# An encoder layer on one core: x also read transposed, the first four attention heads projected ahead of the norm

## The chip, the core and the metric

The kernel runs on one core of a Trainium2 chip. Its time is device time in microseconds (us) from launch to the last byte of the output. Engines are named as in the profile: PE is TensorE (matmuls; PEld is its weight load), ACT is ScalarE, DVE is VectorE, POOL is GpSimd, SP is the queue that issues the DMAs. The profile's clock starts with the span of one profiled execution; what lies between span and measured time is launch and end.

## What is computed

One layer over 256 tokens of 1024 numbers, all in float32. Cut to what matters here:

```python
xn = _rms_norm(x, norm1_g[i])                     # per token: x * rsqrt(mean(x^2)+eps) * gain
(a_x, a_g, b_q, b_k, b_v, c_q, c_kv, c_kpe,
 d_q, d_k, d_v, d_g, gate_logits) = jnp.split(xn @ w_in[i], IN_OFFSETS, axis=-1)
y_a = _rglru_mixer(a_x, a_g, ...)                 # conv, four gates, two linear scans
y_b = _diff_attention(b_q, b_k, b_v, ...)         # 8 heads; q and k are rms-normed per head
y_c = _mla(c_q, c_kv, c_kpe, ...)
y_d = _retention(d_q, d_k, d_v, d_g, ...)
merged = gates[0]*(y_a @ w_br_a) + gates[1]*(y_b @ w_br_b) + ...
x = x + merged @ w_out[i]
x = x + square(relu(_rms_norm(x, norm2_g) @ w_ff1)) @ w_ff2
x = x + sigmoid(_rms_norm(x, norm3_g) @ w_ple_gate) * (p @ w_ple_proj)
```

## The kernel before, in words

**Matmuls.** Every large product is done in three PE passes: both operands are split into a high part (rounded to PE's fp32r form) and a low part, and high*high, high*low and low*high are summed. x is split once into `xTh` and `xTl` (features on partitions). Weights stream from memory in tiles of 1 MB (`raw`, three buffers, `load`, issued on SP). `pieces` turns half a tile at a time into a high part `hi` (a copy on ACT; for some pieces a CAST on DVE) and a low part `lo` (a subtraction on DVE); there are NR = 5 buffers of each. `a_mode` makes 512 columns (or 384, 320) of tokens-by-features from two tiles, `b_mode` 256 features by tokens from one. Both end a tile with a call of `tick`.

**Stages, in program order.** First the norm: `rstd` of x on ACT, a scaling on DVE, 16 PE transposes (line 207 is `transpose`, line 194 is `mm`), the split into `xTh`/`xTl`. Then `a_in(0..3)` (the recurrence's input and its convolution `xc`), `b_in(0)` and `b_in(1)` (q, k, v of four heads each), `a_out(0..3)` (the recurrence's gelu branch; each needs its finished recurrence `ha[u]`), `c_in` (the latent projections: the first matmuls that are 384 columns wide), then gates, merges, the other branches, output, feed-forward and the last gate.

**Side work.** What is not a large product is written as generators: `a_mix(u)` (recurrence block u: gate matmuls `mm<-xc,bd` in plain float32, sigmoids, exp, tanh, square, square root, two scans), `b_rot` (head norm, rotation, transposes), `b_mix` (scores, softmax, weighted sum) and so on. `start` appends one to the list `side`; `tick` adds `pace` units of credit per tile (G0 = 3.0 in the first phase) and advances the first WIDTH = 4 generators whose `needs` are met until the credit is used up; each `yield` states its cost. Per generator these costs add up to 11.5 for an `a_mix`, 2.2 and 2.8 for a `b_rot` of q and of k, 9.8 for a `b_mix`. `finish(g)` runs g to its end at once. In the list the generators stand in the order in which they were started.

**Who orders the queues.** The tile framework places each instruction in its engine's queue by the order of the program, with priorities: loads and pieces are raised by AHEAD and AHEAD_S (60 instructions), the start by FIRST. After that each engine takes its own queue strictly as it stands, and waits on semaphores for what it needs. Accumulators `acc` are four PSUM banks, `mm` four more.

The main program of this phase is:

```python
for u in range(4):
    xc = a_in(u)
    if u == 0:
        derived_params()
    ...
    ga.append(start(a_mix(u, xc, ha[u])))
yb = yhl()
for c in range(2):
    for p, (...) in enumerate(b_in(c)):
        gb.append(start(b_mix(2 * c + p, ...), (r0, r1)))
pace[0] = G1
for u in range(4):
    finish(ga[u])
    a_out(u, ha[u], ya)
cs = c_in()
```

Of the kernel before, what the change touches and what calls it, by code (L numbers as in the profile page):

```python
# [14 lines left out]
P = 128  # L15
# [143 lines left out]
def _pack(w):  # L159
    import numpy as np  # L160

    return {'x': np.asarray(w['x']), 'weights': _pack_weights(w), 'params': _pack_params(w), 'lru': _pack_lru(w),
            'pT': np.ascontiguousarray(np.asarray(w['p'])[0, 0].T.reshape(2, P, S).transpose(1, 0, 2)),
            'gate_b': np.ascontiguousarray(np.asarray(w['gate_b'])[0]), 'decay': _decay()}

# [2 lines left out]
def encoder_kernel(ctx: ExitStack, tc: tile.TileContext, a, out):  # L168
# [50 lines left out]

    xs = const.tile([P, 2, D], F32, name="xs")  # L220
    par = const.tile([P, N_PAR], F32, name="par")
    with tc.high_priority(FIRST):
        for t in range(2):
            for c in range(2):
                w = slice(512 * c, 512 * c + 512)
                nc.sync.dma_start(xs[:, t, w], a['x'][0, t * P:(t + 1) * P, w])
        nc.sync.dma_start(par[:, :O_LATE], a['params'][:, :O_LATE])

    ident = const.tile([P, P], F32, name="ident")
    make_identity(nc, ident)  # L230
# [4 lines left out]
    act(eps[:, 2:3], eps[:, 0:1], AF.Sqrt)  # L235
    nhalf = const.tile([P, 16], F32, name="nhalf")
    nc.vector.memset(nhalf, -0.5)

# [9 lines left out]
    sp = const.tile([P, 2, 16], F32, name="sp")  # L248

    def derived_params():  # L250
        nc.sync.dma_start(par[:, O_LATE:], a['params'][:, O_LATE:])
# [45 lines left out]
    xTh = const.tile([P, 8, S], F32R, name="xTh")  # L297
    xTl = const.tile([P, 8, S], F32R, name="xTl")

    def rstd(src, scratch):  # L300

        st = small.tile([P, 2], F32, tag="nst", name="nst")
# [66 lines left out]
    def pieces(raw, o, n, alloc=None):  # L369
# [5 lines left out]
            hi, lo = alloc(), alloc()  # L375
        with tc.high_priority(AHEAD_S):
            count[0] += 1
            if count[0] % 2 == 0 and count[0] in V_HI:
                nc.vector.tensor_copy(out=hi[:, :n], in_=raw[:, o:o + n])
            else:  # L380
                act(hi[:, :n], raw[:, o:o + n], AF.Copy)
# [9 lines left out]
    def a_mode(xh, xl, name, KT, n0, nn, by_token=0):  # L391
# [4 lines left out]
        for k0 in range(0, KT, 4):  # L396
            kc = min(4, KT - k0)
            raw = load(name, k0 * P, n0)
            for p0 in range(0, kc, 2):
                kp = min(2, kc - p0)  # L400
                hi, lo = pieces(raw, p0 * nn, kp * nn)
                late = k0 >= KT - by_token
                for t in range(2):
# [37 lines left out]
    with tc.tile_pool(name="br", bufs=1) as br:  # L441
# [4 lines left out]
        def SH(name):  # L446
            return br.tile([P, 512], F32, tag="SH", name=name, bufs=NS)

        with tc.high_priority(FIRST):
            for t in range(2):  # L450
                r_ = rstd(xs[:, t, :], lambda: SH("xsq"))
                nc.vector.tensor_scalar(out=xs[:, t, :], in0=xs[:, t, :], scalar1=r_, scalar2=None, op0=MULT)
            for k2 in range(4):
                pt = mm_bank().rearrange("p (k s) -> p k s", s=S)
                for t in range(2):
# [3 lines left out]
                for k in range(2):  # L459
                    kk = 2 * k2 + k  # L460
                    split_scaled(xTh[:, kk, :], xTl[:, kk, :], pt[:, k, :], c1('norm1_g', kk))

        def y4():
            return br.tile([P, 4, S], F32R, tag="y4", name="y4", bufs=NY)
# [129 lines left out]
            split_scaled(*yw(yy, 2 * p), pair_T(lambda t, h: y[:, t, h, :]), gcol)  # L594


        def b_in(c):

            pairs = [[], []]
            for j, o0 in enumerate((O_BQ, O_BK, O_BV)):  # L600
                ps = a_full(xh, xl, W_in, 8, o0 + 512 * c, 512)
                for p in range(2):
                    x = (SH if j < 2 else L)("bx").rearrange("p (t c) -> p t c", t=2)
                    for t in range(2):
                        act(x[:, t, :], ps[t][:, 256 * p:256 * p + 256], AF.Copy)
# [486 lines left out]
```

## Time and profile before

| what | value |
|---|---|
| median of 3 runs | 736.91 us (736.8 to 738.08) |
| the profiled execution's own time | 736.86 us |
| its span | 735.1 us |
| granted TensorE clock, mean | 1.000 |
| PE busy | 718.0 us, 98% |
| DVE busy | 526.6 us, 72% |
| ACT busy | 428.2 us, 58% |
| first `a_out` matmul | 116.73 us |
| first 384-column matmul (`c_in`) | 140.62 us |

The table by engine says how much each engine worked in all; the windows say in which stretch; a timeline row gives start, length, engine, source line, operation, and in brackets how long the engine stood idle before it and what released it. PE lengths are pipelined and overlap, so rates are read from the starts of rows that follow each other.

### The profile page before, as it was taken

The numbers are of one execution on the slowest core, as the hardware profiler recorded it, in microseconds if no ns is written. First come the engines' busy times: TensorE is split into PE (matmuls) and PEld (weight loads), VectorE is DVE, ScalarE is ACT, GpSimd is POOL, SyncE is SP. The second block draws the span as 40 slices with busy tenths as digits, with TensorE's granted clock in tenths as the row PEclk, the third lists the DMA queues.
The fourth block names the chain that finished last, engine by engine and source line by source line (L and its number), as shares of the span: only waits on it lengthen the run. The fifth ranks groups of instructions, "written<-read, shape, count | busy, mean of one in ns | idle before, by whom it ended". The sixth has DMA issues, their size and how long they took to land.

```text
span 735.1 us, 10616 instructions
## 1 busy us (share of the span) xinstructions
PE 718.0 (98%) x4066; PEld 622.7 (85%) x4066; DVE 526.6 (72%) x893; ACT 428.2 (58%) x744; POOL 49.4 (7%) x58
## 2 busy tenths in 40 slices
PE   5999999999999999999999999999999999999997
PEld 4988889997888898888888888877899999888886
DVE  5988978998777879976775778576666666445652
ACT  7589867483745996556544444445755555445551
POOL 0000012222011033110000101000000000000000
PEclk9999999999999999999999999999999999999999
DMA  8754444365344254443555475543564455536611
GB/s 299 263 218 172 171 172 144 119 247 188 122 161 136 91 180 167 170 170 132 186 173 198 163 244 185 199 171 144 179 222 172 173 179 193 202 118 227 233 52 58
DMA packets 22802, 128.47 MB, mean 175 GB/s; under 512 B 2656, under 2 KB 2912, under 8 KB 9440
## 3 DMA queue, kind: packets, MB, share of 16 engines
q1 hardware_dynamic: 22752, 127.80, 48.8%
q8 instruction: 32, 0.52, 0.3%
q14 instruction: 18, 0.15, 0.1%
HBM read 126.74 MB, written 1.05 MB: 174 GB/s over the span
## 4 chain that ended last, share of the span: by engine, by line
PE 64%; DVE 1%; ACT 0%; issue 0%
PE acc L194 57%; PE mm L194 3%; PE mm L207 2%; PE mm L198 1%; ACT hi L191 0%; DVE lo L185 0%; DVE gate L188 0%; DVE pg L185 0%; DVE y L188 0%; DVE xs L185 0%; ACT pg L191 0%
## 5 line engine op out<-in xcount | busy, mean ns | idle before, releaser
L185 DVE TENSOR_TENSOR lo<-raw,hi 128x1024 fp32r<-128x1024 f32 (+3 forms) x226 | 268.3, 1192 | 119.3 <-ACT hi L191 118.8
L191 ACT ACTIVATE hi<-raw 128x1024 fp32r<-128x1024 f32 (+2 forms) x200 | 207.6, 1043 | 194.8 <-PE acc L194 166.0
L194 PE MATMUL acc<-hi,xTh 128*128 128x512 f32 (+3 forms) x376 | 146.3, 389 | 0.0
L194 PE MATMUL acc<-hi,y 128*128 128x512 f32 x448 | 144.5, 398 | 0.0
L194 PE MATMUL acc<-hi,xTl 128*128 128x512 f32 (+3 forms) x376 | 142.8, 380 | 0.0
L194 PE MATMUL acc<-lo,xTh 128*128 128x512 f32 (+3 forms) x376 | 142.6, 379 | 0.0
L194 PE MATMUL acc<-xTl,hi 128*128 128x256 f32 x384 | 109.1, 284 | 0.2 <-DVE xTl L188 0.2
L194 PE MATMUL acc<-xTh,hi 128*128 128x256 f32 x384 | 109.2, 286 | 0.0
L194 PE MATMUL acc<-xTh,lo 128*128 128x256 f32 x384 | 108.7, 284 | 0.0
L194 PEld LDWEIGHTS acc<-hi,y 128*128 128x128 f32 x448 | 84.2, 188 | 19.8
L194 PE MATMUL acc<-lo,y 128*128 128x512 f32 x224 | 89.0, 397 | 0.0
L194 PEld LDWEIGHTS acc<-hi,xTl 128*128 128x128 f32 x376 | 70.6, 188 | 13.1
L194 PEld LDWEIGHTS acc<-hi,xTh 128*128 128x128 f32 x376 | 70.7, 188 | 13.0
L194 PEld LDWEIGHTS acc<-lo,xTh 128*128 128x128 f32 x376 | 70.7, 188 | 12.1
L194 PEld LDWEIGHTS acc<-xTl,hi 128*128 128x128 f32 x384 | 74.0, 193 | 0.7 <-DVE xTl L188 0.5
L194 PEld LDWEIGHTS acc<-xTh,hi 128*128 128x128 f32 x384 | 73.8, 193 | 0.2
L194 PEld LDWEIGHTS acc<-xTh,lo 128*128 128x128 f32 x384 | 73.7, 192 | 0.1
L194 PEld LDWEIGHTS acc<-lo,y 128*128 128x128 f32 x224 | 42.1, 188 | 9.5
L194 PE MATMUL acc<-hi,h 128*128 128x512 f32 x128 | 40.7, 397 | 0.0
L194 PEld LDWEIGHTS acc<-hi,h 128*128 128x128 f32 x128 | 23.9, 188 | 5.6
L194 PE MATMUL acc<-lo,h 128*128 128x512 f32 x64 | 25.3, 395 | 0.0
L194 PE MATMUL acc<-hi,cT 128*128 128x384 f32 (+1 forms) x80 | 24.1, 368 | 0.8 <-ACT cqp L191 0.8
(225 smaller groups left out, 890.0 us busy)
## 6 DMA issues: line engine op xcount, KB each, us to landing
raw<-in_weights_dram SPq DMA_DIRECT2D x104, 1024.0 KB, 4.8
raw<-in_weights_dram SPq DMA_DIRECT2D x6, 512.0 KB, 3.5
raw<-in_weights_dram SPq DMA_DIRECT2D x4, 576.0 KB, 3.7
bd<-in_lru_dram SPq DMA_DIRECT2D x8, 256.0 KB, 5.2
gb<-in_gate_b_dram SPq DMA_DIRECT2D x8, 256.0 KB, 5.0
dec<-in_decay_dram SPq DMA_DIRECT2D x8, 256.0 KB, 5.9
raw<-in_weights_dram SPq DMA_DIRECT2D x2, 768.0 KB, 4.3
raw<-in_weights_dram SPq DMA_DIRECT2D x2, 640.0 KB, 3.6
```

Source lines behind the costliest of these rows:

```text
L185: nc.vector.tensor_tensor(out=o, in0=x, in1=y, op=op)
L191: nc.scalar.activation(o, x, f, **kw)
L194: nc.tensor.matmul(o, lhsT=lhsT, rhs=rhs, start=start, stop=stop)
L198: nc.tensor.matmul(o, lhsT=lhsT, rhs=rhs, start=start, stop=stop, skip_group_check=True)
L207: nc.tensor.transpose(o, x, ident[:x.shape[0], :x.shape[0]])
```

## The change

x is also stored transposed (`xT`) and read first. The q, k and v of heads 0 to 3 (`b_in(0)`) are projected first of all, from this xT times the norm's gain but without the tokens' factors; those multiply q, k and v when they are copied out of PSUM (`scale=r1[t]`). The loads of x itself, its factors, `derived_params` and the transposes to `xTh`/`xTl` become one more generator, `norm1`, which is started ahead of `b_in(0)` and finished behind it; its stated costs add up to 14. The first weight tile is loaded in three parts (one issued by ACT, as are the first parameters), and the first tiles are converted a quarter at a time. Eight matmuls of zeros run on PE at the start. The `b_rot` and `b_mix` of heads 0 to 3 are started before the `a_mix`, which used to stand first in the list. `a_in(0..3)` and `b_in(1)` follow.

```diff
+    raw0 = ring.tile([P, 2048], F32, tag="raw", name="raw", bufs=3)
     with tc.high_priority(FIRST):
-        for t in range(2):
-            for c in range(2):
-                w = slice(512 * c, 512 * c + 512)
-                nc.sync.dma_start(xs[:, t, w], a['x'][0, t * P:(t + 1) * P, w])
-        nc.sync.dma_start(par[:, :O_LATE], a['params'][:, :O_LATE])
+        nc.scalar.dma_start(par[:, :O_LATE], a['params'][:, :O_LATE])
+
+        cold = small.tile([P, P], F32, tag="cold", name="cold", bufs=1)
+        nc.vector.memset(cold, 0.0)
+        pt = mm_bank()
+        for _ in range(WARM):
+            mm(pt[:, 0:P], cold, cold, True, True)
...
-            if count[0] % 2 == 0 and count[0] in V_HI:
+            if count[0] % 2 == 0 and count[0] - 2 in V_HI:
...
-            for p0 in range(0, kc, 2):
-                kp = min(2, kc - p0)
+            fine = 1 if count[0] < 4 else 2
+            for p0 in range(0, kc, fine):
+                kp = min(fine, kc - p0)
...
-        with tc.high_priority(FIRST):
+        r1 = []
+        done = set()
+
+        def norm1():
+
             for t in range(2):
-                r_ = rstd(xs[:, t, :], lambda: SH("xsq"))
-                nc.vector.tensor_scalar(out=xs[:, t, :], in0=xs[:, t, :], scalar1=r_, scalar2=None, op0=MULT)
+                for c in range(2):
+                    w = slice(512 * c, 512 * c + 512)
+                    nc.sync.dma_start(xs[:, t, w], a['x'][0, t * P:(t + 1) * P, w])
+            nc.sync.dma_start(par[:, O_LATE:], a['params'][:, O_LATE:])
+            yield 2.0
+            for t in range(2):
+                r1.append(rstd(xs[:, t, :], lambda: SH("xsq"), 'rst1'))
+                yield 1.5
+            derived_params()
+            yield 3.0
+            for t in range(2):
+                nc.vector.tensor_scalar(out=xs[:, t, :], in0=xs[:, t, :], scalar1=r1[t], scalar2=None, op0=MULT)
+                yield 1.0
...
-        def b_in(c):
+        def b_in(c, x=(xh, xl), pre=None):
...
-                ps = a_full(xh, xl, W_in, 8, o0 + 512 * c, 512)
+                ps = a_full(*x, W_in, 8, o0 + 512 * c, 512)
+                if pre is not None:
+                    while len(r1) < 2:
+                        next(pre)
+                kw = [{} if pre is None else dict(scale=r1[t]) for t in range(2)]
...
+                        act(z[:, t, :], ps[t][:, 256 * p:256 * p + 256], AF.Copy, **kw[t])
...
+        with tc.high_priority(FIRST):
+            o = offs[W_in, 0, O_BQ][0]
+            src = a['weights'][o:o + 512 * 512].rearrange("(p c) -> p c", c=2048)
+            nc.sync.dma_start(x1r[0][:, 0:2], a['xT'][:, 0:2])
+            nc.scalar.dma_start(raw0[:, 0:512], src[:, 0:512])
+            nc.sync.dma_start(raw0[:, 512:1024], src[:, 512:1024])
+            nc.sync.dma_start(x1r[0][:, 2:4], a['xT'][:, 2:4])
+            nc.sync.dma_start(raw0[:, 1024:2048], src[:, 1024:2048])
+            nc.sync.dma_start(x1r[1], a['xT'][:, 4:8])
...
+        yb = yhl()
+        pre = start(norm1())
+        for p, (r0, qT, rq, rk, kT, _, v) in enumerate(b_in(0, (x1k(0), x1k(1)), pre)):
+            gb.append(start(b_mix(p, qT, rq, kT, v, yb), (r0, rk)))
+        finish(pre)
         for u in range(4):
             xc = a_in(u)
-            if u == 0:
-                derived_params()
             ha.append(L("rr").rearrange("p (f s) -> p f s", s=S))
             ga.append(start(a_mix(u, xc, ha[u])))
-        yb = yhl()
-        for c in range(2):
-            for p, (r0, qT, rq, r1, kT, _, v) in enumerate(b_in(c)):
-                gb.append(start(b_mix(2 * c + p, qT, rq, kT, v, yb), (r0, r1)))
+        for p, (r0, qT, rq, rk, kT, _, v) in enumerate(b_in(1)):
+            gb.append(start(b_mix(2 + p, qT, rq, kT, v, yb), (r0, rk)))
```

How the built programs differ, at three places. The first is the start of PE's queue. Before (`xs` is x, `ident` the identity matrix of a transpose, the `acc` that follows is `a_in(0)`):

```order
L207 MATMUL mm_114<-ident_77,xs_70 128x128 x4
L207 MATMUL mm_123<-ident_77,xs_70 128x128 x4
L207 MATMUL mm_132<-ident_77,xs_70 128x128 x4
L207 MATMUL mm_141<-ident_77,xs_70 128x128 x4
L194 MATMUL acc_151<-xTh_93,hi_154 128x256
```

and now, also on PE, from the zeros (`cold`) on (`y4_105` is the high part of the first half of xT, `acc_122` and `acc_123` are q of the two token halves):

```order
L197 MATMUL mm_76<-cold_74 128x128 x8
L197 MATMUL acc_122<-hi_124,y4_105 128x512
L197 MATMUL acc_122<-lo_125,y4_105 128x512
L197 MATMUL acc_123<-hi_124,y4_105 128x512
L197 MATMUL acc_123<-lo_125,y4_105 128x512
L197 MATMUL acc_122<-hi_124,y4_106 128x512
```

The 16 transposes are gone from the head of the queue; the first projection stands right behind the zeros.

The second place is ACT's queue in the stretch of `a_out`. Before, from the first piece of `a_out(2)` (`hi_1331`) over that of `a_out(3)` (`hi_1415`) to the first two of `c_in` (`hi_1502`, `hi_1554`), with `gel` the gelu of `a_out` and `rr` the one square root of the recurrence that is still left:

```order
L191 ACTIVATE hi_1331<-raw_1329 128x1024
L191 ACTIVATE rr_1036<-rr_1036,eps_82 128x512
L191 ACTIVATE hi_1415<-raw_1413 128x1024
L191 ACT_TABLE_LOAD
L191 ACTIVATE gel_1249<-acc_1176 128x512
L191 ACTIVATE y4_1172<-gel_1249 128x512
L191 ACTIVATE hi_1502<-raw_1500 128x768
L191 ACTIVATE gel_1323<-acc_1254 128x512
L191 ACTIVATE y4_1172<-gel_1323 128x512
L191 ACTIVATE bsq_1402<-bx_742 128x512
L191 ACTIVATE hi_1554<-raw_1552 128x768
```

and now, from the last copies of v (`bx_1298<-acc_1176`, the end of `b_in(1)`) over the first piece of `a_out(2)` (`hi_1588`) on; `rr_565`, `rr_1286` and the `aa` belong to `a_mix(0)`:

```order
L194 ACTIVATE bx_1298<-acc_1176 128x256
L194 ACTIVATE bx_1301<-acc_1176 128x256
L194 ACTIVATE hi_1588<-raw_1586 128x1024
L194 ACTIVATE rr_1286<-mm_1288,par_71 128x256 x2
L194 ACTIVATE ii_1287<-mm_1293,par_71 128x256 x2
L194 ACT_TABLE_LOAD
L194 ACTIVATE aa_1308<-rr_565,sp_99 128x256 x2
L194 ACTIVATE rr_565<-rr_565,sp_99 128x256 x2
L194 ACTIVATE sq_1313<-aa_1308 128x512
L194 ACTIVATE aa_1317<-rr_1286,sp_99 128x256 x2
L194 ACTIVATE rr_1286<-rr_1286,sp_99 128x256 x2
```

Before, the recurrence was all but over at `a_out`; now its first block has only begun there, and the three others stand behind it.

The third place is ACT's queue ahead of the first piece of `c_in`, which is `hi_1809` now; `rr_826`, `rr_1675`, `aa` and `sq` belong to `a_mix(3)`, the last block:

```order
L194 ACT_TABLE_LOAD
L194 ACTIVATE aa_1687<-rr_826,sp_99 128x256 x2
L194 ACTIVATE rr_826<-rr_826,sp_99 128x256 x2
L194 ACTIVATE sq_1692<-aa_1687 128x512
L194 ACTIVATE aa_1696<-rr_1675,sp_99 128x256 x2
L194 ACTIVATE rr_1675<-rr_1675,sp_99 128x256 x2
L194 ACTIVATE sq_1701<-aa_1696 128x512
L194 ACT_TABLE_LOAD
L194 ACTIVATE rr_826<-rr_826,eps_90 128x512
L194 ACTIVATE rr_1675<-rr_1675,eps_90 128x512
L194 ACTIVATE hi_1809<-raw_1807 128x768
```

From `bx_1298<-acc_1176` to `hi_1809`, both counted, ACT's queue now holds 108 instructions: 16 table loads, 28 sigmoids (`rr<-mm`, `ii<-mm`), 32 exp and tanh (`aa`, `rr<-rr,sp`), 8 squares, 8 square roots, 3 gelus, 3 copies `y4<-gel`, 2 copies `y4<-mm`, 3 squares `bsq`, 2 copies of v and 3 weight pieces. All of `a_mix(1)` to `a_mix(3)`, and `a_mix(0)` from the middle of its gates, moved to between these two points.

More of the change, by code (lines that the diff above doesn't have):

```diff
@@ L28 @@
 V_HI = range(8, 60)
+WARM = 8
 O_AX, O_AG, O_BQ, O_BK, O_BV = 0, 1024, 2048, 3072, 4096
@@ L160, in _pack @@
     import numpy as np
-    return {'x': np.asarray(w['x']), 'weights': _pack_weights(w), 'params': _pack_params(w), 'lru': _pack_lru(w),
+    return {'x': np.asarray(w['x']),
+            'xT': np.ascontiguousarray(np.asarray(w['x'])[0].T.reshape(8, P, S).transpose(1, 0, 2)), 'weights': _pack_weights(w), 'params': _pack_params(w), 'lru': _pack_lru(w),
             'pT': np.ascontiguousarray(np.asarray(w['p'])[0, 0].T.reshape(2, P, S).transpose(1, 0, 2)),
@@ L233, in encoder_kernel @@
         nc.vector.memset(eps[:, j:j + 1], v)
-    act(eps[:, 2:3], eps[:, 0:1], AF.Sqrt)
     nhalf = const.tile([P, 16], F32, name="nhalf")
@@ L250, in derived_params @@
     def derived_params():
-        nc.sync.dma_start(par[:, O_LATE:], a['params'][:, O_LATE:])
         gr = par[:, O_GR:O_LAM].rearrange("p (j c w) -> p j c w", j=2, c=2)
@@ L298, in encoder_kernel, with rstd @@
     xTl = const.tile([P, 8, S], F32R, name="xTl")
-    def rstd(src, scratch):
-        st = small.tile([P, 2], F32, tag="nst", name="nst")
+    def rstd(src, scratch, tag="nst"):
+        st = small.tile([P, 2], F32, tag=tag, name="nst", bufs=4 if tag == "nst" else 2)
         sq = scratch()
@@ L359, in encoder_kernel @@
     count = [0]
+    early = {}
     def load(name, r0, n0):
+        if (name, r0, n0) in early:
+            return early.pop((name, r0, n0))
         o, (_, _, rows, _, nn, mode) = offs[name, r0, n0]
@@ L461, in encoder_kernel @@
                     split_scaled(xTh[:, kk, :], xTl[:, kk, :], pt[:, k, :], c1('norm1_g', kk))
+                yield 1.0
         def y4():
@@ L594, in y_to_T @@
             split_scaled(*yw(yy, 2 * p), pair_T(lambda t, h: y[:, t, h, :]), gcol)
-        def b_in(c):
+        def b_in(c, x=(xh, xl), pre=None):
             pairs = [[], []]
             for j, o0 in enumerate((O_BQ, O_BK, O_BV)):
-                ps = a_full(xh, xl, W_in, 8, o0 + 512 * c, 512)
+                ps = a_full(*x, W_in, 8, o0 + 512 * c, 512)
[3 more added lines that the diff above has]
+                kw = [{} if pre is None else dict(scale=r1[t]) for t in range(2)]
                 for p in range(2):
-                    x = (SH if j < 2 else L)("bx").rearrange("p (t c) -> p t c", t=2)
+                    z = (SH if j < 2 else L)("bx").rearrange("p (t c) -> p t c", t=2)
                     for t in range(2):
-                        act(x[:, t, :], ps[t][:, 256 * p:256 * p + 256], AF.Copy)
+                        act(z[:, t, :], ps[t][:, 256 * p:256 * p + 256], AF.Copy, **kw[t])
                     if j < 2:
@@ L608, in b_in @@
                         ss = small.tile([P, 2, 4], F32, tag="brs", name="brs", bufs=8)
-                        pairs[p] += [start(b_rot(j, x, dst, ss)), dst, ss]
+                        pairs[p] += [start(b_rot(j, z, dst, ss), () if pre is None else (pre,)), dst, ss]
                     else:
-                        pairs[p].append(x)
+                        pairs[p].append(z)
             return pairs
@@ L940, in encoder_kernel, with x1k, get @@
         ha, ga, gb, gc = [], [], [], []
+        x1 = yhl()
+        early[W_in, 0, O_BQ] = raw0
+        x1r = [y4().bitcast(F32) for _ in range(2)]
+        with tc.high_priority(FIRST):
[7 more added lines that the diff above has]
+            nc.sync.dma_start(x1r[1], a['xT'][:, 4:8])
+            act(eps[:, 2:3], eps[:, 0:1], AF.Sqrt)
+        def x1k(i):
+            def get(k):
+                if k not in done:
+                    done.add(k)
+                    with tc.high_priority(FIRST if k == 0 else AHEAD_S + 20):
+                        split_scaled(x1[k // 4][0][:, k % 4, :], x1[k // 4][1][:, k % 4, :], x1r[k // 4][:, k % 4, :],
+                                     c1('norm1_g', k))
+                return x1[k // 4][i][:, k % 4, :]
+            return get
+        yb = yhl()
[3 more added lines that the diff above has]
+        finish(pre)
         for u in range(4):
             xc = a_in(u)
-            if u == 0:
-                derived_params()
             ha.append(L("rr").rearrange("p (f s) -> p f s", s=S))
             ga.append(start(a_mix(u, xc, ha[u])))
-        yb = yhl()
-        for c in range(2):
-            for p, (r0, qT, rq, r1, kT, _, v) in enumerate(b_in(c)):
-                gb.append(start(b_mix(2 * c + p, qT, rq, kT, v, yb), (r0, r1)))
+        for p, (r0, qT, rq, rk, kT, _, v) in enumerate(b_in(1)):
+            gb.append(start(b_mix(2 + p, qT, rq, kT, v, yb), (r0, rk)))
         pace[0] = G1
```

## The prediction

> **What bounds the kernel now.** I read the windows first, cut where a stage begins (start:end, length; then busy time and instructions of PE, PEld, DVE, ACT, POOL; granted clock; DMA share; GB/s).
>
> ```profile
> 0.00:7.40 7.40, 0.00 (x0) 0.00 (x0) 1.21 (x6) 4.04 (x10) 0.69 (x6) 1.00 0.71 233
> 7.40:12.38 4.98, 3.56 (x16) 3.19 (x17) 2.41 (x7) 2.99 (x8) 0.00 (x0) 1.00 1.00 414
> 12.38:15.01 2.63, 2.46 (x13) 2.09 (x11) 2.62 (x7) 2.63 (x6) 0.00 (x0) 1.00 1.00 421
> 15.01:116.73 101.72, 101.72 (x538) 88.50 (x539) 87.22 (x148) 80.41 (x144) 1.86 (x2) 1.00 0.55 196
> 116.73:140.60 23.87, 23.87 (x203) 23.87 (x202) 22.05 (x37) 12.77 (x22) 7.10 (x6) 1.00 0.36 122
> 140.60:735.10 594.50, 586.39 (x3305) 505.04 (x3303) 411.11 (x692) 325.33 (x559) 39.70 (x44) 1.00 0.48 169
> ```
>
> PE is busy without a gap from 15.01 to 140.60 (101.72 of 101.72, 23.87 of 23.87), and nearly so behind that. So PE's own work sets the time there, and a delay of ACT, DVE or a load costs nothing until PE has run out of what was prepared for it. In the stretch of `a_out` (116.73 to 140.60) ACT works only 12.77 of 23.87 us. At the head PE waits. Its waits (total, times, longest) and its timeline (start, length) say for what:
>
> ```profile
> PE mm L207 <- DVE xs L452: 8.8, 2, 7.4
> PE mm L207 <- DVE cT L188: 1.4, 1, 1.4
> ```
>
> ```profile
> 7.44 0.66 PE L207 MATMUL mm<-ident,xs 128*128 128x128 f32 x2 [7.44 <-DVE xs L452]
> 9.48 3.25 PE L207 MATMUL mm<-ident,xs 128*128 128x128 f32 x14 [1.39 <-DVE xs L452]
> 12.38 0.56 PE L194 MATMUL acc<-xTh,hi 128*128 128x256 f32 x1
> ...
> 14.16 0.28 PE L194 MATMUL acc<-xTl,hi 128*128 128x256 f32 x1
> 14.28 0.27 PE L194 MATMUL acc<-xTh,lo 128*128 128x256 f32 x1
> 14.46 0.39 PE L194 MATMUL acc<-xTh,hi 128*128 128x256 f32 x1
> 15.01 0.39 PE L194 MATMUL acc<-xTl,hi 128*128 128x256 f32 x1 [0.17 <-DVE xTl L188]
> ...
> 116.14 0.39 PE L194 MATMUL acc<-hi,xTl 128*128 128x512 f32 x1
> 116.38 0.60 PE L207 MATMUL mm<-ident,bx 128*128 128x128 f32 x4
> 116.73 0.36 PE L194 MATMUL acc<-xTh,hi 128*128 128x256 f32 x1
> ```
>
> ```profile
> 341.04 1.75 PE mm L207 x16
> ```
>
> The wait for x (`xs`, scaled on DVE) is 8.8 of the first 9.5 us. Before 15.01 PE has done 16 transposes, which take 1.75 us at full rate (the row of the chain), and ten matmuls of 256 columns, 0.12 us each at full rate (14.16 to 14.28), 1.2. So 15.0 - 3.0 = 12.1 us of the head are lost. I call V the end of `b_in(1)`'s last matmul, 116.38 here, where `a_out` follows.
>
> **The change: prices.** ACT's timeline, groups (count | busy us, mean ns | idle before), a DVE timeline, PE groups (two records for each gate product), and the page's DMA issues (KB, us to landing):
>
> ```profile
> 108.22 1.28 ACT L191 ACT_TABLE_LOAD   x1
> 109.51 0.91 ACT L191 ACTIVATE aa<-rr,sp 128x256 f32<-128x256 f32 x2
> ...
> 113.77 1.04 ACT L191 ACTIVATE hi<-raw 128x1024 fp32r<-128x1024 f32 x1
> 114.83 1.28 ACT L191 ACT_TABLE_LOAD   x1
> 116.12 0.72 ACT L191 ACTIVATE rr<-rr,eps 128x512 f32<-128x512 f32 x1
> 116.75 0.62 ACT L191 ACTIVATE bsq<-bx 128x512 f32<-128x512 f32 x1
> 117.27 0.67 ACT L191 ACTIVATE bT<-mm,par 128x512 fp32r<-128x512 f32 x1
> ...
> 118.36 1.19 ACT L191 ACTIVATE bx<-acc 128x256 f32<-128x256 f32 x4
> 119.42 1.08 ACT L191 ACTIVATE hi<-raw 128x1024 fp32r<-128x1024 f32 x1
> 120.37 0.75 ACT L191 ACTIVATE rr<-rr,eps 128x512 f32<-128x512 f32 x1
> ```
>
> ```profile
> L191 ACT ACT_TABLE_LOAD x18 | 23.1, 1283 | 3.0 <-DVE bsm L185 2.0 <-PEq L1082 0.7
> L191 ACT ACTIVATE ii<-mm,par 128x256 f32<-128x256 f32 x16 | 6.8, 488 | 0.0
> L191 ACT ACTIVATE y<-gel 128x512 fp32r<-128x512 f32 x4 | 2.5, 633 | 11.4 <-DVE gel L185 11.4
> ```
>
> ```profile
> 116.24 1.22 DVE L185 TENSOR_TENSOR lo<-raw,hi 128x1024 fp32r<-128x1024 f32 x1
> 117.38 0.69 DVE L185 TENSOR_TENSOR ii<-ii,rr 128x512 f32<-128x512 f32 x1
> ...
> 118.65 1.22 DVE L555 TENSOR_TENSOR_SCAN rr<-aa,ii 128x512 f32<-128x512 f32 x1
> ```
>
> ```profile
> L194 PE MATMUL mm<-xc,bd 128*128 128x256 f32 x64 | 14.8, 379 | 0.0
> L194 PE MATMUL mm<-bx,baT 128*128 128x128 f32 x64 | 8.3, 275 | 0.0
> L194 PE MATMUL mm<-bT 64*128 64x256 f32 x96 | 8.2, 294 | 0.4 <-ACT be L191 0.4
> ```
>
> ```profile
> raw<-in_weights_dram SPq DMA_DIRECT2D x104, 1024.0 KB, 4.8
> raw<-in_weights_dram SPq DMA_DIRECT2D x6, 512.0 KB, 3.5
> ```
>
> **The head.** Now the first product needs xT and two weight tiles (raw0, raw1), 3 x 1.05 = 3.15 MB, before its last pieces. At the windows' rates 233 GB/s bring 1.72 MB by 7.40, and 414 GB/s the other 1.43 MB by 10.8. Landing comes later: 512 KB more take 4.8 - 3.5 = 1.3 us, so of 4.8 us some 2.2 are no transfer; the part ahead of the bytes is in the first window already, and of 0 to 2.2 I take 1.4: raw1 at 12.2. Then a high piece of 1.06 (113.77 to 114.83) and a low one of 1.22: 14.5. By then PE can have done the 26 matmuls of raw0 and raw1's first pieces, 26 x 0.23 (116.14 to 116.38, 512 columns) = 6.0. So 8.5 us are lost, and 0.5 more for small stalls: 9.0 in place of 12.1, **3.1 us saved**.
>
> x's 16 transposes come later, at the same 1.75. From there to V PE's work is even: out go 24 of 32 gate products, 14.8 x 24/32 = 11.1; in come `b_mix` of two of four pairs, half of 8.3 and half of 8.2, and 28 transposes at 1.75/16: 11.3. So V comes at 116.4 - 3.1 + 0.2 = **113.5**.
>
> The factors now multiply q, whose copies out of PSUM stand at about 25 us and hold back ACT's pieces of the next tiles if late. x stands on SP behind three weight tiles, 5.2 MB, at 414 GB/s by 16; its square, its root and one table load have 9 us. I count that covered; without the cover it would be 1 to 3 us of PE standing still. Moving `derived_params` into this costs PE nothing for the same reason.
>
> The eight zeros: from 12.38 on matmuls of 256 columns step by over 0.2, and only from 14.16 by 0.12, though the granted clock reads 1.00 in all windows; that is 4.7 us after 9.48. At half the rate the 26 matmuls would still end some 0.5 us behind 14.5 at most, so the zeros are worth 0 to 0.5 us; I take 0. The Trainium skill, "TensorE: Matmul & The Clock Gate", in its part on the clock gate, has full rate after a window of about 3.4 us of steady work and loses it after an idle one; by it eight short matmuls followed by a wait need not warm PE, and the sum would be up to 0.5 us later.
>
> **Where `a_mix` goes.** The credits decide. Before, the four `a_mix` (4 x 11.5 = 46) stood first in the list, and the 16 ticks of `a_in` and `b_in` give 48: they were through at `a_out(0)`. Now the six ticks of `b_in(0)` (18) go to `norm1` (14), and the ten left (30) to four `b_rot` (10) and two `b_mix` (19.6), which stand ahead. So `finish(ga[u])` runs each `a_mix` in one piece ahead of its `a_out(u)`, and nearly all of it comes behind V. In ACT's queue 108 instructions now stand from the copies of v, which wait for V, to `hi_1809`, the first piece of `c_in`. By steps from start to start: 16 table loads, 1.29 each (108.22 to 109.51), are 20.6. Four blocks of exp, tanh and square, 4.26 each (109.51 to 113.77), are 17.0. 28 sigmoids at 0.488 less an overlap of 0.10 to 0.12 (as 116.75 + 0.62 reaches past 117.27) are 10.4. Eight roots at 0.63 (116.12 to 116.75) are 5.0. Three squares `bsq` at 0.52, two `y4<-mm` and three gelus, priced as bT at 0.67 - 0.10, and three `y4<-gel` at 0.633 - 0.10 are 6.0. Two pieces at 0.95 (119.42 to 120.37), one of three quarters at 0.8, and two copies of v at 1.06/4 (118.36 to 119.42) are 3.2.
>
> That is 62.2. ACT's waits for DVE's `gel` were 11.4 for four, so 0 to 8.6 for three; I take 3.1, nearer to the lower end, since the gelu now stands well behind most of its block's DVE work. Eight or so instructions end before a table load starts instead of overlapping it, 0.1 each: 1.0. So `hi_1809` ends at V + 66.3. On DVE its low piece stands behind the last product (0.69), two scans (1.22 each): V + 69.5, then `c_in` runs on.
>
> From V to there PE has the 23.9 us it had (116.73 to 140.60), 24 gate products, 11.1, and ten transposes, 1.1: 36.1. It **stands still for 33.4 us**, in gaps ahead of the later `a_out` and of `c_in`; `hi_1717`, the piece of `a_out(3)`, is the 65th of the 108, at about V + 46. SP's later weight loads wait behind the `bd` of the last blocks; none of them is needed before `c_in` begins.
>
> **The sum.** From `c_in` to the end were 594.5. Out go two pairs' `b_mix`, already done, 8.2, and 38 transposes, 4.1; and the stall for `cT` (1.4) with ACT rid of the blocks it was late from; DVE's backlog adds 1. Left: 581.8. Span: 113.5 + 69.5 + 581.8 = 764.8. The profiled execution took 736.86 for its span of 735.1, so 1.8 lie outside, and that is the median (736.91) within 0.1. **767 us**, 4% slower.
>
> **Rivals.** *Faster:* `a_mix` hides behind PE as it did, and only the head counts: 736.9 - 3.1 + 0.2 = 734. It decides if ACT's work from V to `c_in` stays under PE's 36.1 us there; ACT had 11.1 us free in that stretch, and my count is 62. The order of ACT's queue speaks against it: 0.03. *Less:* the queue costs PE only what it does up to `hi_1717` (46 us against about 30 of PE work, 16 lost), and work prepared behind that covers the rest: 749. No `c_in` piece stands ahead of the last block, which speaks against it: 0.07. *More:* the waits for DVE reach 8.6 (+5.5), and DVE, with gates' products and scans between its pieces, stays a further twelve low pieces late through `c_in` and the gates (12 x 1.14, 14): 786. DVE's 22.05 of 23.87 us in `a_out` speak for it: 0.07. *A dearer switch:* each load with about as much again behind it, 16 x 1.4 = 22: 789. The row of 109.51 speaks against it, a start 1.29 behind the load's. The Trainium skill, "ScalarE: Activation LUTs", "What ACT_TABLE_LOAD costs", gives 1283 ns, as here, and a drain of about 1380 ns for each switch, which this trace doesn't show. 0.02. *No change:* the pile-up is small and eats the head's gain, 737: 0.01.
>
> **The numbers.** The forecast has 0.80. Its own bounds are the waits (-3, +5.5), landing (-1, +1), remainder (+-3); the range reaches into the lesser and the larger case: 752 to 786. A measurement of this kernel tells about 0.2%, 1.5 us, from no change. Faster 0.03, same 0.01, slower 0.96.
>
> **What would show it.** Right: the first 512-column matmul well ahead of 12 us, the second tile's last low piece at about 14.5; the first `a_out` matmul at about 113; then gaps of PE with ACT as releaser, the first 384-column matmul at about 183; 23 table loads in place of 18, and ACT nearly full from 113 to 180. Wrong: PE busy through this stretch, or the last scans done by V; then the credits were read wrongly. If ACT is full there but the gaps differ, a price or the waits for DVE are at fault; if V isn't at 113, the head; if the part behind `c_in` isn't 582, the remainder.

## The result and the profile after

The changed kernel takes 768.44 us (median of 5 runs, 768.1 to 769.4) where the kernel before takes 736.91 (736.71 to 738.08): a ratio of 1.0425, interval 1.0412 to 1.0438. It is slower by 31.5 us. The forecast was 767.

First the windows of the changed kernel, cut at its own stage ends: the first product at 7.79, the return of full rate at 12.22, the first `a_out` matmul at 115.61, the first `c_in` matmul at 179.53 (columns as in the prediction).

```profile
0.00:7.79 7.79, 3.79 (x17) 3.49 (x17) 1.36 (x8) 3.09 (x6) 0.68 (x6) 1.00 0.72 234
7.79:12.22 4.43, 4.43 (x10) 3.48 (x11) 4.43 (x11) 3.78 (x9) 0.00 (x0) 1.00 1.03 419
12.22:15.61 3.39, 3.39 (x16) 2.75 (x15) 2.37 (x3) 2.61 (x3) 0.00 (x0) 1.00 0.99 393
15.61:115.61 100.00, 99.94 (x601) 87.08 (x600) 87.97 (x190) 57.71 (x129) 10.79 (x12) 1.00 0.55 199
115.61:179.53 63.92, 41.31 (x260) 37.83 (x258) 39.73 (x71) 62.25 (x107) 5.66 (x6) 0.84 0.15 52
179.53:766.50 586.97, 578.18 (x3185) 496.86 (x3184) 394.76 (x625) 310.57 (x509) 27.42 (x34) 0.99 0.49 173
```

The stretch of `a_out` was 23.9 us long and is 63.9 now. ACT went from 12.77 of 23.87 us to 62.25 of 63.92: it has become the engine that sets this stretch. PE is busy for only 41.31 us, and some of that at a lower clock. Ahead of it ACT has become idle: 57.71 of 100.00 us, where it had 80.41 of 101.72. The work has moved from one window into the other.

PE's waits (total, times, longest), the three largest and two that a later section needs; before, none but the head's was over 1.4 us:

```profile
PE mm L210 <- DVE bx L188: 7.2, 1, 7.2
PE mm L197 <- ACT rr L194: 6.4, 1, 6.4
PE acc L197 <- ACT hi L194: 6.0, 1, 6.0
...
PE mm L210 <- DVE cpp L188: 1.4, 2, 1.2
...
PE mm L210 <- DVE cT L191: 0.2, 1, 0.2
```

Their places in PE's timeline are three rows, ahead of the gate products of the last block (`a_mix(3)`), of `a_out(3)` and of `c_in`:

```profile
148.86 5.42 PE L197 MATMUL mm<-xc,bd 128*128 128x256 f32 x16 [6.43 <-ACT rr L194]
160.29 0.58 PE L197 MATMUL acc<-xTh,hi 128*128 128x256 f32 x1 [6.01 <-ACT hi L194]
177.18 2.37 PE L210 MATMUL mm<-ident,bx 128*128 128x128 f32 x10 [7.16 <-DVE bx L188]
```

The last row names DVE and `bx`. DVE had little to do there. The `bx` is a rotated q of heads 4 to 7, which stands in DVE's queue behind a product of the last block, and that one waits for ACT's square `sq`:

```profile
176.13 0.69 DVE L191 SCALAR_TENSOR_TENSOR rr<-sq,rr 128x512 f32<-128x512 f32 x1 [0.44 <-ACT sq L194]
176.75 0.28 DVE L188 TENSOR_TENSOR bx<-ropea,ropeb 128x128 f32<-128x128 f32 x1
```

ACT's own timeline ahead of `c_in` is the last block and nothing else, row upon row without idle time:

```profile
171.76 0.91 ACT L194 ACTIVATE aa<-rr,sp 128x256 f32<-128x256 f32 x2
...
176.12 1.28 ACT L194 ACT_TABLE_LOAD   x1
177.41 1.33 ACT L194 ACTIVATE rr<-rr,eps 128x512 f32<-128x512 f32 x2
178.65 0.83 ACT L194 ACTIVATE hi<-raw 128x768 fp32r<-128x768 f32 x1
```

The `hi` at 178.65 is the first piece of `c_in`. On DVE its low piece stands behind two scans:

```profile
179.43 2.33 DVE L579 TENSOR_TENSOR_SCAN rr<-aa,ii 128x512 f32<-128x512 f32 x2
181.68 0.93 DVE L188 TENSOR_TENSOR lo<-raw,hi 128x768 fp32r<-128x768 f32 x1
```

### The profile page after: what moved, and what is told of

Its sections match the earlier page's. It is cut to its first block, busy times and chain, and to the rows that moved or that the text cites. A ratio compares the mean times of both kernels' runs of the same rounds, so it can differ in the third digit from the quotient of the medians.

```text
span 766.5 us, 10700 instructions
## 1 busy us (share of the span) xinstructions
PE 731.0 (95%) x4082; PEld 631.5 (82%) x4082; DVE 530.6 (69%) x904; ACT 440.0 (57%) x759; POOL 44.6 (6%) x58
## 4 chain that ended last, share of the span: by engine, by line
PE 68%; DVE 7%; ACT 2%; issue 1%; POOL 1%
PE acc L197 62%; PE mm L197 3%; PE mm L210 2%; DVE lo L188 2%; PE mm L201 1%; ACT hi L194 1%; DVE bsm L680 0%; POOL crq L294 0%; DVE be L191 0%; POOL crk L294 0%; ACT rr L194 0%; DVE hi L386 0%; DVE ii L188 0%; DVE brs L646 0%; DVE csc L750 0%
## 5 line engine op out<-in xcount | busy, mean ns | idle before, releaser
L188 DVE TENSOR_TENSOR lo<-raw,hi 128x1024 fp32r<-128x1024 f32 (+4 forms) x228 | 268.5, 1184 | 140.6 <-ACT hi L194 139.9
L194 ACT ACTIVATE hi<-raw 128x1024 fp32r<-128x1024 f32 (+4 forms) x202 | 207.4, 1034 | 210.3 <-PE acc L197 172.3
L197 PE MATMUL acc<-hi,y 128*128 128x512 f32 x544 | 177.1, 402 | 3.0 <-ACT y L194 3.0
L197 PE MATMUL acc<-hi,xTh 128*128 128x512 f32 (+3 forms) x328 | 126.8, 388 | 0.0
L197 PEld LDWEIGHTS acc<-hi,y 128*128 128x128 f32 x544 | 103.4, 190 | 28.2 <-ACT y L194 3.3
L197 PE MATMUL acc<-lo,xTh 128*128 128x512 f32 (+3 forms) x328 | 124.9, 381 | 1.7 <-DVE lo L188 1.7
L197 PE MATMUL acc<-hi,xTl 128*128 128x512 f32 (+3 forms) x328 | 124.8, 380 | 0.0
L197 PE MATMUL acc<-lo,y 128*128 128x512 f32 x272 | 109.0, 401 | 0.0
L197 PEld LDWEIGHTS acc<-xTl,hi 128*128 128x128 f32 x384 | 74.4, 194 | 0.2
L197 PEld LDWEIGHTS acc<-lo,xTh 128*128 128x128 f32 x328 | 62.3, 190 | 12.5 <-DVE lo L188 2.1
L197 PEld LDWEIGHTS acc<-lo,y 128*128 128x128 f32 x272 | 51.8, 191 | 11.9
```

What stands on the lines that cost most here:

```text
L188: nc.vector.tensor_tensor(out=o, in0=x, in1=y, op=op)
L194: nc.scalar.activation(o, x, f, **kw)
L197: nc.tensor.matmul(o, lhsT=lhsT, rhs=rhs, start=start, stop=stop)
```

## The experiments

Twelve kernels. Each time stands beside that of the kernel before on the same chip (736.8 to 737.4).

**1. The place in the list.** One line puts each `a_mix` ahead of the `b_rot` and `b_mix`:

```diff
             ga.append(start(a_mix(u, xc, ha[u])))
+            side.insert(u, side.pop())
```

> The changed kernel with one line more: each a_mix, when it is started, is put ahead of the b_rot and b_mix in the list, where it stood before the change. Theory (ACT's queue): only 20 instructions and 4 table loads then stand in ACT's queue from v's copies to the first c_in piece, 13 us of them against over 24 us of PE work, so PE doesn't stand still from b_in(1) to c_in and the time falls by all of the 33 us, to 735 +-2: before's 736.9 less the 2 us of the head. Rival (the projection order, the late loads on SP or DVE cost the time, wherever a_mix stands): 750 to 768.

Measured: 745.67 (ratio 1.0113, 1.0096 to 1.0130). Of the 31.5 us, 23 go with this line, so the place in the list is most of it. But 735 was expected, and 8 us over the kernel before are left. PE's largest waits behind the head are at the second weight tile of `c_in` (the profiled execution took 747.91):

```profile
150.24 0.83 ACT L194 ACTIVATE hi<-raw 128x768 fp32r<-128x768 f32 x1
```

```profile
151.12 1.01 PE L197 MATMUL acc<-hi,xTh 128*128 128x384 f32 x2 [3.70 <-ACT hi L194]
```

The expectation had counted ACT's queue up to the first piece of `c_in`, and that count was right: 20 instructions with 4 loads, and the first 384 columns at 141.36 without a wait. The last block, once more run at the end, stands behind that piece and ahead of the second one, the `hi` at 150.24, for whose low piece PE then waits 2.8 us more. It is run at the end because the six ticks of `b_in(0)` come before the first `a_mix` exists: the ten that are left pay 30 of the 46 units of the four blocks.

**2. The order of the projections alone.** The kernel before, in which `b_in(0)` stands ahead of `a_in` (with `derived_params` behind its q). The norm stays first.

```diff
+        yb = yhl()
+        for p, (...) in enumerate(b_in(0)):
+            gb.append(start(b_mix(p, qT, rq, kT, v, yb), (r0, r1)))
         for u in range(4):
             xc = a_in(u)
...
-        for c in range(2):
-            for p, (...) in enumerate(b_in(c)):
+        for p, (...) in enumerate(b_in(1)):
```

> The kernel before with one part of the change alone: b_in(0) and its b_rot and b_mix stand ahead of a_in and a_mix; x is not read transposed, the norm stays ahead of all, there are no zeros. Theory (credits): without the 14 units of norm1 the a_mix get 18 units more ahead of V, so ACT's queue from v's copies to c_in holds 69 instructions and 10 table loads, 39 us by the same prices, 45 with waits and DVE's end, against 36 us of PE work: 9 us of standing still, 747 +-4, so slower than before without xT. Rival (the slowdown comes with xT, the late x or norm1): 737 +-2.

Measured: 759.63 (1.0307, 1.0292 to 1.0323). Slower without xT, norm1 or zeros, so the rival is out. The size was missed by 13 us. The queue was as counted, 69 instructions with 10 loads, but the count again ended at the first piece of `c_in`. The rest of the last block stands behind it, and PE waits a second time, ahead of the 320 columns:

```profile
164.29 2.16 PE L207 MATMUL mm<-ident,bx 128*128 128x128 f32 x8 [11.68 <-DVE bx L185]
179.83 0.86 PE L194 MATMUL acc<-hi,xTh 128*128 128x320 f32 x2 [3.52 <-ACT hi L191]
```

The first gap is 2.7 us longer than the 9 that were expected; the second, with 1.8 for its low piece, was not in the sum.

**3. Fewer table loads.** `a_out` takes a sigmoid in the place of its gelu; the gelu is left out of the computation.

```diff
-            act(gel, ps, AF.Gelu_apprx_tanh)
+            act(gel, ps, AF.Sigmoid)
```

> The changed kernel with a sigmoid in the place of a_out's gelu (the gelu is left out). The a_mix stay behind V, but six table loads go from the stretch ahead of c_in (10 in place of 16); c_in's first piece moves ahead of the last block's roots. Theory (ACT's queue is what PE waits for, a load is 1.29 us): 7.7 us less for the loads, up to 5 more from the moved roots: 755 to 761. Rival (a switch costs 2.66 us): 747 to 753. Rival (DVE, the gate products or SP's loads set the end of the stretch): 766 to 768.4.

Measured: 762.46 (1.0342, 1.0326 to 1.0357), 6.0 less than the changed kernel and 1.5 outside what was expected. The rows of ACT and of PE at `c_in` say more than the total. The first piece of `c_in` on ACT, and the matmul with which `c_in` runs on:

```profile
165.46 0.83 ACT L194 ACTIVATE hi<-raw 128x768 fp32r<-128x768 f32 x1
```

```profile
171.59 0.69 PE L197 MATMUL acc<-lo,xTh 128*128 128x384 f32 x1 [4.10 <-DVE lo L188]
```

In the changed kernel they are at 178.65 and 182.66. So ACT's piece comes 13.2 us earlier, 0.5 of them because V does (113.56), where the same prices as in the prediction give 12.1 (six loads, the two roots and part of the last block, which now stand behind that piece); with a drain of the load's own length behind each load it would be some 20. PE runs on 11.1 us earlier: ACT's queue sets the stretch, and a load costs about its 1.29 us here. Four us of the span are given back later (759.4 - 171.6 against 766.5 - 182.7), where the rest of the last block stands among the pieces of `c_in`.

**4. `a_out` later.** The changed kernel with the loop over `finish(ga[u])` and `a_out(u)` moved from ahead of `c_in` to behind `gates(0)`.

> The changed kernel with the four a_out, and the finish ahead of each, moved behind c_in and the first gates. The list and the credits stay. Theory: no a_mix is run at once ahead of c_in, so PE has c_in and the gates to do while ACT works through the 62 us; most of the standing still goes: 737 to 747. Rival (what costs the time lies in c_in or in b_mix itself): above 760.

Measured: 756.35 (1.0261, 1.0245 to 1.0276). It gives 12 us, not 21 to 31. PE has work through `c_in` and the gates, and then waits, at one place:

```profile
204.43 1.94 PE L210 MATMUL mm<-ident,bx 128*128 128x128 f32 x8 [13.64 <-DVE bx L188]
```

Only two of the four blocks had been worked off in the meantime: they still stand behind the others in the list, and `finish` ran the last two in one piece all the same, later (on ACT from 172.90 on). The time lies between the two forecasts. It is nearer to the rival's, but `c_in` and `b_mix`, which the rival meant, are not what PE waits for.

**5 and 6. More credits, a_mix first.** As run 1, with G0 = 5.0 and 6.0 in place of 3.0.

> The kernel with a_mix first in the list (e1_mix_first) and G0 = 5.0 in place of 3.0. Theory (credits): of the 46 units of the four a_mix the ten ticks of a_in and b_in(1) paid only 30 at 3.0, so the last block was still run at once ahead of a_out(3); at 5.0 they pay 50, the last block is through before V, and the 8.6 us that PE loses around the first c_in matmuls go: 737 +-2. Rival (the loss at c_in comes from DVE, whatever is paid before): 743 to 746.

> As the run before, with G0 = 6.0: room for the b_rot and a b_mix of the first heads too. Theory: PE loses nothing between b_in(1) and c_in, and the head's 2 us show: 735 +-2. Rival (DVE, busy 84 of 96 us ahead of V at 3.0, can't take more side work, and the pieces come late there): 740 or more.

Measured: 746.32 (1.0127, 1.0113 to 1.0141) and 750.03 (1.0173, 1.0159 to 1.0187). Here the theory fell: paying for the blocks ahead of V does not make the time fall. The windows of the run with 6.0 from 40 to 120:

```profile
40.00:60.00 20.00, 19.89 (x148) 18.65 (x147) 18.24 (x39) 8.25 (x16) 9.43 (x8) 1.00 0.52 182
60.00:80.00 20.00, 20.00 (x130) 18.44 (x129) 18.99 (x33) 14.44 (x29) 0.00 (x0) 1.00 0.57 206
80.00:100.00 20.00, 20.00 (x92) 16.96 (x91) 11.33 (x19) 19.86 (x40) 0.00 (x0) 1.00 0.36 132
100.00:120.00 20.00, 17.44 (x72) 13.70 (x71) 13.75 (x19) 19.87 (x33) 0.00 (x0) 0.91 0.23 79
```

From 80 on ACT is full, and the weight pieces of `b_in(1)` and `a_out` queue behind blocks that are now issued too close together; PE's stalls only move from `c_in` to 113 and 125. From 40 to 60 ACT works 8.25 of 20 us, with no block to work on. The kernel before, in the same two windows:

```profile
40.00:60.00 20.00, 20.00 (x91) 16.83 (x90) 15.70 (x25) 19.82 (x39) 0.00 (x0) 1.00 0.57 205
60.00:80.00 20.00, 20.00 (x90) 16.64 (x89) 18.09 (x23) 18.18 (x34) 0.00 (x0) 1.00 0.48 164
```

It fills ACT there, with blocks, because its `a_in` comes first.

**7. More credits, the list as changed.** The changed kernel with G0 = 6.0.

> The changed kernel, list order and all, with G0 = 6.0 alone. More credits carry part of the a_mix ahead of V: ACT's queue from v's copies to the first c_in piece holds 70 instructions and 11 loads in place of 108 and 16, 43 us by the same prices in place of 62. Theory: 20 us less, 748 +-6. Rival (it is the order of the list that counts, not the credits): 765 to 769.

Measured: 764.99 (1.0375, 1.0361 to 1.0389). It gives 3.5 us, not 20, so the rival's number was right. The queue was as counted, 70 instructions with 11 loads, and yet the first `c_in` piece comes only 4.5 us earlier on ACT (178.65 in the changed kernel). PE stands still in one gap ahead of it:

```profile
174.13 0.83 ACT L194 ACTIVATE hi<-raw 128x768 fp32r<-128x768 f32 x1
```

```profile
172.66 2.37 PE L210 MATMUL mm<-ident,bx 128*128 128x128 f32 x10 [19.48 <-DVE bx L188]
```

Two things had been left out of the count. One is that the counted stretch begins later: the gate products that the credits moved ahead of V take PE's time there, so V comes at 120.5 in place of 114.07; and the last copies of v, which have blocks ahead of them in ACT's queue, come at 123.8 in place of 114.3. The other is that ACT waits 7.2 us in the stretch, 4.2 of them at 164.21 for a `gel`; on DVE this stands behind a `bx` that had waited 4.9 us for POOL's `brs`. A price list of one engine's queue doesn't hold such waits.

**8. More zeros.** As run 6, with 24 zeros in place of 8.

> As the run before with 24 zeros in place of 8. In the changed kernel the eight zeros end at 4.8 us, PE idles 3.0 us and its first ten matmuls run at 0.43 us in place of 0.23. Theory: zeros up to the first product keep the clock, 2.0 us less than with 8, unless raw1's pieces are late then (0.5 to 1 less of the gain). Rival (the rate at the start hangs on something else): no difference, +-1.

Measured: 749.31 against 750.03, 0.7 less, with intervals (1.0149 to 1.0177 and 1.0159 to 1.0187) that overlap. In the trace the rate did change. With 8 zeros the first products step by 0.43 us; with 24 they step by 0.23 from the second on:

```profile
8.48 0.48 PE L197 MATMUL acc<-hi,y 128*128 128x512 f32 x1
8.80 0.40 PE L197 MATMUL acc<-lo,y 128*128 128x512 f32 x1
9.04 0.63 PE L197 MATMUL acc<-hi,y 128*128 128x512 f32 x2
...
13.96 0.63 PE L197 MATMUL acc<-hi,y 128*128 128x512 f32 x2
14.72 0.50 PE L197 MATMUL acc<-lo,y 128*128 128x512 f32 x1
```

The zeros show where the rate changes: in 1.5 us PE takes 9 of their records up to 5.5 us, and 15 or 16 from there on. Eight zeros end at 4.8, short of it. And yet PE reaches the first product of `a_in` only 0.64 us earlier (44.38 in place of 45.02): the 24 zeros run into the first product, which could start at 7.99 and starts at 8.48, and PE now waits for the second tile's low piece, at 14.72 (0.76 behind two matmuls that take 0.46).

**9 to 11. An earlier start.** As run 1; first with v of heads 0 to 3 behind `a_in` (only their q and k come first), then instead with `a_out` behind `c_in` and the gates as in run 4, then with both.

```diff
-        for p, (...) in enumerate(b_in(0, (x1k(0), x1k(1)), pre)):
-            gb.append(...)
+        b0 = b_in(0, (x1k(0), x1k(1)), pre, (0, 1))
         finish(pre)
         for u in range(4):
...
+        for p, (...) in enumerate(b_in(0, (x1k(0), x1k(1)), pre, (2,), b0)):
+            gb.append(...)
```

> The kernel with a_mix first in the list (G0 = 3.0), in which only q and k of heads 0 to 3 come first; a_in follows, and their v comes behind a_in. With a_mix first ACT still ran out: in the two runs with more credits it was busy 19.9 of 20 us from 80 on, but only 8.3 of 20 from 40 to 60, since no a_mix exists before the first a_in is done. Theory (late start): a_in comes 11 us earlier, ACT gets 11 us more of the stretch in which it idles, and most of the 8.6 us at c_in goes: 738 +-2. Rival (ACT's whole work is too much, whenever it starts): 744 to 747.

> The kernel with a_mix first in the list (G0 = 3.0) and the four a_out behind c_in and the first gates. Theory (late start): ACT has the 30 us of PE work in c_in and the gates more before anything waits for the last block, the 8.6 us at c_in go, and with the head's 1 to 2 us the time is 736 +-2. Rival (the late b_rot and b_mix of heads 4 to 7 are what PE waits for then, as when a_out was moved alone): 742 to 750.

> Both of the two moves before: v of heads 0 to 3 behind a_in, a_out behind c_in and the gates, a_mix first. Theory: 735 +-2, the head's gain and no new wait of ACT. Rival (the table loads that the finer mixing adds eat it): 740 or more.

Measured: 741.04 (1.0054, 1.0041 to 1.0066), 743.49 (1.0093, 1.0079 to 1.0107), 741.71 (1.0069, 1.0055 to 1.0083). An earlier `a_in` is worth 4.3 us against run 1 (by the ratios), and 741.04 is the lowest of all variants; none beats the kernel before. The first run lies between its theory and its rival; the last two came out some 5 us above the theory's range, and the rivals' numbers came true. With `a_out` moved away no wait of PE over 0.8 us is left between the head and 240 us, and a part of the lost time turns up behind it, where PE waits for the latent branch's `cqp` (2.4 us at 274 in the one, 4.4 at 256 in the other); why it is late was not traced. The table loads are 28 and 29 in the runs with v later and 20 in the middle one, so their number alone doesn't order the times. But the kernel before has 18, and ten more at 1.28 us are 13 us of ACT's time: as a part of what is left, the rival of the last run is not excluded.

**12. A late start alone.** The kernel before, with its own order, norm and list, in which the blocks are only started when `b_in(0)` is through:

```diff
-            ga.append(start(a_mix(u, xc, ha[u])))
+            ga.append(a_mix(u, xc, ha[u]))
...
                 gb.append(start(b_mix(2 * c + p, ...), (r0, r1)))
+            if c == 0:
+                for u in range(4):
+                    start(ga[u])
+                    side.insert(u, side.pop())
```

> The kernel before, with its order of products, its norm and its list (a_mix first), but the four a_mix are only started when b_in(0) is done; the head is before's. It does nothing but to start them later. Theory (late start): in the runs so far the time rises with the moment at which the first a_mix gets to ACT (first of its ii at 33 us: 737; 54: 741 to 742; 65 to 67: 743 to 750; 75: 760; 109: 768). Here only the six ticks of b_in(1), 18 of 46 units, come ahead of V; 28 are left, between the 16 left in the run with a_mix first (746) and the 46 of the changed kernel (768): 750 to 758. Rival (the order of the projections, xT or the zeros cost the time, not the start of a_mix): 736 to 739.

Measured: 761.88 (1.0331, 1.0313 to 1.0350), 24.4 us slower, and 4 over what was expected. ACT from 40 to 80, and PE's wait at `c_in`:

```profile
40.00:60.00 20.00, 20.00 (x90) 16.57 (x89) 17.07 (x30) 7.43 (x15) 5.49 (x4) 1.00 0.68 239
60.00:80.00 20.00, 20.00 (x94) 16.67 (x93) 16.01 (x26) 7.42 (x12) 5.07 (x4) 1.00 0.53 194
```

```profile
166.63 1.01 PE L194 MATMUL acc<-hi,xTh 128*128 128x384 f32 x2 [11.50 <-ACT hi L191]
```

No other part of the change is in this kernel. ACT idles for 25 of 40 us where it was nearly full, and the same work has to be done later, in front of PE. The run doesn't part two things: ten of the sixteen ticks are also gone when the blocks start, so `finish` runs more of them in one piece. All runs with `a_out` at its place and the full computation, by the start of the first `ii` on ACT, with ACT's busy time in the 100 us from 16 to 116 and its table loads:

| kernel | first `ii` on ACT, us | ACT busy, us of 100 | table loads | time, us |
|---|---|---|---|---|
| before | 33.3 | 78.7 | 18 | 736.9 |
| a_mix first, v later | 54.8 | 80.1 | 28 | 741.0 |
| a_mix first, G0 = 6.0, 24 zeros | 65.8 | 75.6 | 22 | 749.3 |
| a_mix first, G0 = 5.0 | 65.9 | 74.4 | 24 | 746.3 |
| a_mix first, G0 = 6.0 | 66.3 | 75.3 | 22 | 750.0 |
| a_mix first | 67.7 | 71.7 | 24 | 745.7 |
| before, b_in(0) first | 74.7 | 61.5 | 24 | 759.6 |
| before, blocks held back | 85.0 | 54.8 | 23 | 761.9 |
| the list as changed, G0 = 6.0 | 93.9 | 63.4 | 20 | 765.0 |
| changed | 109.8 | 57.7 | 23 | 768.4 |

The late starts (from 74.7 on) go with 15 to 24 us less of ACT's work by 116 us, and with 760 to 768. Among the four that start at 66 to 68, none of these columns orders the times. The run at 54.8 has lost nothing of ACT's busy time by 116 us and is still 4 us slower, so the idle time of ACT does not account for all of it.

## Why the prediction was right, point by point

**The head: smaller than forecast, for another reason.** Forecast were 9.0 us lost in place of 12.1, with raw1's last low piece at 14.5 as the limit. Measured is a first product at 7.79, and ten matmuls that take 4.43 us (12.22 - 7.79) in place of 2.3: 7.8 + 2.1 = 9.9 lost, 2.2 saved. What failed is the sentence that by 14.5 PE can have done the 26 matmuls, 6.0 us at full rate, and with it that the zeros cost nothing. PE never had to wait for raw1. The head of PE's timeline, from the zeros on:

```profile
1.03 3.78 PE L197 MATMUL mm<-cold 128*128 128x128 f32 x16 [1.03 <-DVE eps L239]
7.79 0.80 PE L197 MATMUL acc<-hi,y 128*128 128x512 f32 x1 [2.97 <-ACT y L194]
...
12.22 0.47 PE L197 MATMUL acc<-lo,y 128*128 128x512 f32 x1
```

The zeros end at 4.81, PE idles 2.97 us, and the products start at half rate. By the clock gate's rule in the Trainium skill ("TensorE: Matmul & The Clock Gate", the part on the clock gate: a window of about 3.4 us of work before full rate), eight zeros of 3.78 us with a gap behind them need not be enough, and the trace agrees: full rate comes 4.4 us after 7.79. So the step that failed is the rate of the first matmuls. It cost 0.9 us against the forecast, of which run 8, with PE at full rate, got back some 0.6: there PE waits for the second tile's low piece, the limit that the prediction had named.

V came at 114.07, not at 113.5, and that it is so near is in part luck. Not 24 gate products left the stretch ahead of V but 28: of the 64 records, eight start before 114.07. At the trace's step of 0.215 us a record these are 12.0 us and not 11.1; so what came in must be some 11.9 in place of 11.3, and the two errors nearly cancel.

**The credits and the queue: right.** From V to the end of `hi_1809` the prediction had 66.3 us; measured are 65.4 (114.07 to 179.48). To its low piece 69.5; measured 68.5 (182.61). `hi_1717` was to end at V + 46 and ends at V + 46.2 (160.23); by ACT's rows it is the 77th of the 108, not the 65th, and it is for the 77th that the prediction's prices give some 46. The first `a_out` matmul is at 115.61 and not at 113, behind gate products of the first block, and the first of 384 columns at 179.53; the one at 182.66 is that with which `c_in` runs on. ACT's prices held; the rows had been taken from the same kind of work:

```profile
L194 ACT ACT_TABLE_LOAD x23 | 29.5, 1283 | 2.3 <-PEq L1137 1.6 <-DVE bsm L188 0.3
```

The waits for `gel` were the main unknown; ACT waited for it 0.8 and 0.4 us inside the stretch (1.67 us idle in all, 63.92 - 62.25), less than the 3.1 taken. PE's work at full rate was put too low, at 36.1 us: with 28 gate products it is 37.0. So of 114.07 to 182.66 PE lost 31.6 us where 33.4 were forecast, and not all in gaps as the prediction has it: its gaps are 24.3, and the rest is work at half rate behind them.

**The remainder: 2.0 too short.** Forecast 581.8; from 182.66 to the end are 583.8. After the gaps PE works at half rate again:

```profile
182.66 0.69 PE L197 MATMUL acc<-lo,xTh 128*128 128x384 f32 x1 [1.69 <-DVE lo L188]
183.15 0.52 PE L197 MATMUL acc<-hi,xTl 128*128 128x384 f32 x1
183.47 0.52 PE L197 MATMUL acc<-hi,xTh 128*128 128x384 f32 x1
...
186.58 0.33 PE L197 MATMUL acc<-lo,xTh 128*128 128x384 f32 x1
186.76 0.33 PE L197 MATMUL acc<-hi,xTl 128*128 128x384 f32 x1
```

0.32 us a step up to 186, 0.18 from 186.58: about twelve matmuls at 0.15 more are 1.8 us, a term that the sum did not have. Of the stalls, that for `cT` fell from 1.4 to 0.2 as counted, those for `cqp` (0.8) and `be` (0.4) went, and one of 1.4 for `cpp` came; only the first was in the sum.

**The sum.** 114.1 + 68.6 + 583.8 = 766.5 where 113.5 + 69.5 + 581.8 = 764.8 stood. The errors of three terms, +0.6, -0.9 and +2.0, are each a few tenths of a per cent, and partly cancel, as those inside the first one do.

**What the prediction did not see.** It took the list's order and the credits for the cause, and by that a faster kernel was one line away. Run 1 says that this is 23 of 31 us, runs 5 and 6 that more credits don't bring the rest, and run 12 that a start behind `b_in(0)` alone costs 24 us (the parts overlap and can't be added): a block can't go to ACT before its `a_in` is done. Even with the blocks first in the list the first `ii` comes 34 us later than before (67.7 and 33.3). The rows gave reason for doubt: ACT's 80.41 of 101.72 us ahead of V, which the prediction quotes, leave 21 us of room. How the rest comes about is shown in part only. In run 1 ACT has worked 7 us less than before by 116 us, and has six table loads more, 7.7 us; in run 9 it has worked as long as before, and has ten loads more behind that. No run takes these loads away, so they stand as an untested rival beside the late start. Whether some order holds both the head's gain and a full ACT stays open too. The lowest time tried is 741.04; in it PE still idles 1.8 us around `c_in` (busy for 18.17 of 20 us from 140 to 160), and where the rest goes was not traced.

## What to carry to other kernels

When a tuned kernel is reordered to fill an idle head, look at what the moved stage used to feed: the engine that idles most in a stretch may be one whose work has to be produced early. A stall that a queue will cause can be summed from the rows of the kernel before, here to within some 5% (31.6 us where 33.4 were forecast), if the order of the queue is known and every table load in it is counted. But count past the first instruction that matters: in runs 1 and 2 the count was right and the next piece, behind it, was the one that PE waited for. And raising a budget did not help an engine that was full; a window of run 1 (ACT 19.86 of 20 us from 80 to 100) shows that it was full there before runs 5 and 6.

## What the runs showed of the hardware

The rate after a gap. Behind 3.0 us of idle PE at the head, ten matmuls at 0.43 in place of 0.23 us; behind the gaps of 7.2 and 1.7 us at `c_in`, 3.5 us at half rate (to 186). Behind the gap of 1.2 us at 129.31 full rate was back after one record. At the start, with zeros from 1.03 on without a gap, it doubles between 5.2 and 5.5 us (run 8). The granted clock of the profile showed half rate in the stretch of the gaps (0.84 from 115.61 to 179.53) and not at the head (1.00 from 7.79 to 12.22), while in run 1 it reads 0.50 from 8 to 13 for the same steps; so the steps, not that column, tell a cold PE.

A table load. In ACT's full queue the next activation starts 1.29 us behind the start of a load (176.12 and 177.41), and run 3, with six loads fewer ahead of `c_in`, agrees with that price and not with one of twice the length.
